# A conditioning dot product for two feature blocks at once: 256 moving columns per product in the first stage of a two-layer diffusion backbone

## The chip, the core and the metric

The kernel runs on one core of a Trainium2 chip. The core has a matrix engine (TensorE, PE in the profile; its weight loads are PEld), an elementwise and reduction engine (VectorE, DVE), an activation engine (ScalarE, ACT), GpSimd (POOL) and SyncE (SP), which here only issues DMAs. They run beside each other and wait for one another by semaphores. The metric is the device time of one execution in microseconds; lower is better.

## The reference

Two layers over 256 latent tokens and 256 context tokens of 2048 features, all in fp32. Each half-layer is modulated by a vector of conditions c (and c_ctx for the context tokens):

```python
sh1, sc1, g1, sh2, sc2, g2 = ada_params(c[:, None, :], ada_w[i], ada_b[i])   # silu(c) @ w + b, in six parts
a  = modulate(h, sh1, sc1)                                                   # h * (1 + scale) + shift
ac = modulate(hc, csh1, csc1)                                                # context: the same weights, c_ctx
q, k, v = jnp.split(a @ w_qkv, 3, axis=-1)                                   # layer 0: neighbourhood attention
```

What matters here is the very beginning: before any key, query or value of layer 0 can be computed, a block of 128 features of the tokens needs its scale (SC1) and shift (SH1): for each of the block's 128 output features a dot product of 2048 terms with silu(c) and another with silu(c_ctx). SC1 and SH1 together are 2 x 2048 x 2048 weights, 32 MB that are read once.

## The kernel before

**Tiling.** The 512 tokens (256 latent, 256 context) are the moving columns, the 2048 features are cut in 16 blocks `kt` of 128. A product of two fp32 matrices is made of three products of rounded parts (`mm3`, L85 to L88): high x high, high x low, low x high; `split_into` (L90) makes the high part on ScalarE (L91) and the low part on VectorE (L92). Weights come through `prefetch` and `piece` (L104, L125): a raw tile (four buffers), then its high and low part (three buffers each).

**The first stage** is the loop over `kt` from L395, about the first 150 us. For each block it adds the block's share to the keys of three heads (`keys`, nine products of 512 columns) and to the values of four heads (`values`, twelve). From `kt` 3 to 14 it also makes an early part of the keys of other heads, twelve products into a bank of their own (`eps`, L444), which VectorE then copies or adds into SBUF (L449, L453). In between, the loop prepares the modulation of a block two ahead (`ahead`): `fetch` loads weights of the conditioning and the block's tokens `xt`; `dots` makes the dot products; `rows` calls `gather`; `modulate` makes tmp = xt * scale + shift on ScalarE (L368) and splits it into `ah` and `al`, the operands of that block's keys and values.

**The dots.** For blocks 0 to 3 TensorE makes both vectors, for blocks 4 to 15 (from `DVE0`) it makes SC1 and VectorE makes SH1. On TensorE (`dot`, L336) the stationary operand is a piece of silu(c) and silu(c_ctx), two columns padded to 32, and the moving one the weights, 128 inputs x 128 outputs; the sixteen products of one block and vector are spread over four strips of 32 columns of the array (`tile_position`) that add up in four groups of 32 partitions of the tile `aps`. `gather` (L349) copies this to SBUF (`row`), adds up the four groups and turns the rows into columns with one small product per vector (L356, with `sel`), and VectorE adds the bias (L358) into `mod`. On VectorE (`dot_dve`, L327) two multiply-and-sum instructions of 128x2048 (L331, for c_ctx and c) and one addition (L334) make SH1 from weights stored the other way round (`ada_s`).

**Buffers and order.** A piece of conditioning weights is 1 MB and takes one of four tiles in turn (`slots`, by the count `n % 4`); its load can be issued when the tile's last reader is done. `aps` and `eps` share one PSUM bank (tag "a", one buffer): each waits until the one before it was read. The order on TensorE in this loop and the loads of `load_st` and `load_x` are fixed in program order (`pin`); from iteration 2 on the loads of `prefetch` are not, and the order of most instructions on VectorE and ScalarE is laid out by the framework's scheduler when the program is built. All loads named here are issued on SP's queue.

Of the kernel before, what the change touches and what calls it, by code (L numbers as in the profile page):

```python
# [2 lines left out]

# [1 line left out]

# [9 lines left out]
ALU = mybir.AluOpType  # L15
# [3 lines left out]
P = 128  # L19
D = 2048  # L20
NT = 256
KT = D // P
# [22 lines left out]
DVE0 = 4  # L45
# [7 lines left out]
def hybrid_kernel(ctx: ExitStack, tc: tile.TileContext, i, out):  # L53
# [213 lines left out]
    with tc.tile_pool(name="attnX", bufs=1) as px, ExitStack() as late:  # L267
# [21 lines left out]
        with tc.tile_pool(name="st", bufs=1) as st:  # L289
# [3 lines left out]
            def load_st(src, name, n):  # L293
                pool, tag, bufs = slots[n % 4]
                r = pool.tile([P, 2048], F32, tag=tag, name=name, bufs=bufs)
                pin(nc.sync.dma_start(r, src))
                return r

            held = {}

            def fetch(kt):
                for t in range(2):
                    src = i["ada_s"][kt - DVE0] if t and kt >= DVE0 else i["ada_p"][kt, t]
                    held[kt, t] = load_st(src, f"ap{kt}{t}", 2 * kt + t)
                load_x(kt)

            zero = st.tile([P, 512], F32, tag="zero", name="zero")
# [16 lines left out]

            raw_c = st.tile([P, KT, 2], F32, tag="rawc", name="raw_c")

            def dot_dve(kt, t):  # L327
                r = held.pop((kt, t))
                junk = outer.tile([P, D], BF16, tag="ada", name=f"junk{kt}", bufs=ADA)
                for n, (o, bc) in enumerate(((junk, cc_bc), (r, c_bc))):  # L330
                    V.scalar_tensor_tensor(  # L331
                        o, r, 1.0, bc, ALU.mult, ALU.mult, accum_out=raw_c[:, kt, 1 - n : 2 - n]
                    )
                V.tensor_scalar(mod[:, 1, kt, :], raw_c[:, kt, :], badj[:, 0, SH1, kt : kt + 1], None, ALU.add)  # L334

            def dot(kt, t):  # L336
                if t and kt >= DVE0:
                    return dot_dve(kt, t)
                if t == 0:
                    dps[kt] = stp_pool.tile([P, 512], F32, tag="a", name=f"aps{kt}")  # L340
                r = held.pop((kt, t))
                for kk in range(KT):
                    g = 32 * (kk % 4)
                    pin(T.matmul(
                        dps[kt][g : g + 32, t * P : (t + 1) * P], c_pad[:, kk, :], r[:, kk * P : (kk + 1) * P],
                        start=kk < 4, stop=kk >= KT - 4, tile_position=(0, g),
                    ))

            def gather(kt):  # L349
                ps = dps.pop(kt)  # L350
                ts = 1 if kt >= DVE0 else 2
                row = st.tile([P, 2 * P], F32, tag="row", name=f"row{kt}", bufs=1)
                S.copy(row[:, 0 : ts * P], ps[:, 0 : ts * P])
                o = ps[:, 256:260].rearrange("p (t b) -> p t b", t=2)
                for t in range(ts):
                    pin(T.matmul(o[:, t, :], row[:, t * P : (t + 1) * P], sel, start=True, stop=True))  # L356
                for t, ada in enumerate((SC1, SH1)[:ts]):
                    V.tensor_scalar(mod[:, t, kt, :], o[:, t, :], badj[:, 0, ada, kt : kt + 1], None, ALU.add)  # L358

            def load_x(kt):  # L360
                xt[kt] = st.tile([P, 512], F32, tag="xt", name=f"xt{kt}", bufs=3)
# [33 lines left out]
            for kt in range(KT):  # L395
                hi, lo = piece()
                first, last = kt == 0, kt == KT - 1

                def keys(h):
                    c = slice(h * P, (h + 1) * P)  # L400
                    mm3(kps[h], hi[:, c], lo[:, c], ah[:, kt, :], al[:, kt, :], first, last, pin)

                def values(b):
                    c, tb = slice(HK0 * P, W0), slice(b * P, (b + 1) * P)
                    mm3(vps[b], ah[:, kt, tb], al[:, kt, tb], hi[:, c], lo[:, c], first, last, pin)

                def dots(k):
                    if k < KT:
                        if k > 2:
                            fetch(k)  # L410
                        for t in range(2):
                            dot(k, t)

                def rows(k):
                    if k < KT:
                        gather(k)

                ahead = kt + 2 if kt > 1 else kt + 1
                keys(0)
                if kt == 2:  # L420
                    rows(3)
                    modulate(3)
                keys(1)
                keys(2)
                dots(ahead)
                values(0)
                values(1)
                rows(ahead)
                values(2)
                values(3)  # L430
                if kt == 0:
                    modulate(1)
                    for bc in (c_bc, cc_bc):
                        pin(S.activation(bc, bc, AF.Silu))
                    fetch(2)
                if kt == 1:
                    modulate(2)
                    dots(3)
                    pos["bufs"], pos["pin"] = 3, False
                for at, h, k0 in EARLY:  # L440
                    if at == kt:
                        h += HK0
                        hi, lo = piece()
                        ps = stp_pool.tile([P, 512], F32, tag="a", name=f"eps{h}{k0}")  # L444
                        for j in range(EN):
                            c = slice(j * P, (j + 1) * P)
                            mm3(ps, hi[:, c], lo[:, c], ah[:, k0 + j, :], al[:, k0 + j, :], j == 0, j == EN - 1, pin)
                        if h in early:
                            V.tensor_tensor(early[h], ps, early[h], ALU.add)  # L449
                        else:  # L450
                            free = NH - 2 * (h - HK0 + 1)
                            early[h] = oT[:, free : free + 2, :].rearrange("p a b -> p (a b)")
                            V.tensor_copy(early[h], ps)  # L453
                if 2 < kt and kt + 1 < KT:
                    modulate(kt + 1)
# [513 lines left out]
    ffn(1, m, (1, G2), "d1", store, free, True)  # L969


def dot_keys():
    keys = []
    for layer, ts in ((0, (SH2, SC2, G1, G2)), (1, (SH1, SC1, G1, SH2, SC2, G2))):
        keys += [(layer, t, nt) for t in ts for nt in range(KT)]
    return keys
# [35 lines left out]
def lay_out(x, c, ctx, c_ctx, ada_w, ada_b, ln_g, ln_b, na_w_qkv, na_w_o, na_rpb,  # L1012
            gm_w_in, gm_ln_g, gm_ln_b, gm_w_s, gm_b_s, gm_w_out, ffn_w_in, ffn_w_out):
    a = {}
    x, ctx = x[0], ctx[0]
    rows = np.stack([c[0], c_ctx])
    a["c_rows"] = rows
    a["c_col"] = rows.reshape(2, KT, P).transpose(2, 1, 0)
    xc = np.concatenate([x, ctx], 0)
    a["xcT"] = xc.T.reshape(KT, P, 512)  # L1020
    a["x_tok"] = x.reshape(2, P, D).transpose(1, 0, 2)
    a["ada_b_col"] = ada_b.reshape(2, 6, KT, P).transpose(3, 0, 1, 2)
    g4, b4 = ln_g.reshape(4, D), ln_b.reshape(4, D)
    a["ln_row"] = np.stack([g4, b4], 1)
    a["ln_col"] = a["ln_row"].reshape(4, 2, KT, P).transpose(3, 0, 1, 2)
    aw = ada_w.reshape(2, D, 6, D)
    dot = np.empty((len(DOT), P, D), np.float32)
    for (layer, t, nt), n in DOT.items():
        dot[n] = aw[layer, :, t, nt * P : (nt + 1) * P].T
    a["ada_t"] = dot  # L1030
    a["ada_p"] = np.stack(
        [[aw[0, :, t, kt * P : (kt + 1) * P].reshape(KT, P, P).transpose(1, 0, 2).reshape(P, 2048)
          for t in (SC1, SH1)] for kt in range(KT)]
    )
    a["ada_s"] = np.stack([aw[0, :, SH1, kt * P : (kt + 1) * P].T for kt in range(DVE0, KT)])
    wq, wk, wv = (na_w_qkv[0][:, n * D : (n + 1) * D] for n in range(3))
    w0 = np.concatenate([wk[:, : HK0 * P], wv[:, :512]], 1)
    a["w_kv0"] = w0.reshape(KT, P, W0)

    a["ident"] = np.eye(P, dtype=np.float32)  # L1040
    a["sel"] = np.tile(np.eye(32, 2, dtype=np.float32), (4, 1))

    a["w_q"] = heads(wq)
    a["w_k"] = heads(wk)[HK0:]
    a["w_v"] = blocks_512(wv)[1:]
    a["bias"] = bias_layout(na_rpb[0])
    a["w_o"] = halves(na_w_o[0])
    parts = ffn_w_in.reshape(2, D, 2, DFF)
    a["w_in_t"] = np.stack([[blocks_512(parts[n, :, p]) for p in range(2)] for n in range(2)])
    a["w_out"] = np.stack([halves(w) for w in ffn_w_out])  # L1050
    a["w_gin"] = blocks_512(gm_w_in[0])
    a["w_gout"] = halves(gm_w_out[0])
    a["gm_row"] = np.stack([gm_ln_g[0], gm_ln_b[0]])
    a["w_s"] = gm_w_s[0].transpose(2, 0, 1)
    a["b_s"] = gm_b_s[0].T
    return {k: np.ascontiguousarray(v) for k, v in a.items()}
# [17 lines left out]
```

## Time and profile before

| what | us |
|---|---|
| median of three runs | 2400.17 (2398.44 to 2400.63) |
| the profiled execution | 2400.89 |
| its span (first to last instruction) | 2399.1 |
| TensorE busy in the first 150 us | 142.93 |
| VectorE busy in the first 150 us | 103.20 |
| DMA share of the first 150 us | 0.92 at 342 GB/s |

Times in the views are from the start of the span; L344 is line 344 of the kernel before. In a row of the timeline stand the start, the length, the engine, the line and operation, out<-in with shapes, how many instructions were merged, and in brackets how long the engine was idle before and what released it. An fp32 product is recorded as two matmuls and two weight loads; a product of the rounded parts is one. Matmuls overlap: the distance from one start to the next says more than the length of one.

### The profile page before, as it was taken

The numbers are of one execution on the slowest core, as the hardware profiler recorded it, in microseconds if no ns is written. First come the engines' busy times: TensorE is split into PE (matmuls) and PEld (weight loads), VectorE is DVE, ScalarE is ACT, GpSimd is POOL, SyncE is SP. The second block draws the span as 40 slices with busy tenths as digits, with TensorE's granted clock in tenths as the row PEclk, the third lists the DMA queues.
The fourth block names the chain that finished last, engine by engine and source line by source line (L and its number), as shares of the span: only waits on it lengthen the run. The fifth ranks groups of instructions, "written<-read, shape, count | busy, mean of one in ns | idle before, by whom it ended". The sixth has DMA issues, their size and how long they took to land.

```text
span 2399.1 us, 31422 instructions
## 1 busy us (share of the span) xinstructions
PE 2370.2 (99%) x11628; PEld 1969.3 (82%) x11628; DVE 1716.8 (72%) x2297; ACT 1121.9 (47%) x1546; POOL 57.4 (2%) x63
## 2 busy tenths in 40 slices
PE   8999999999999999999999999999999999999998
PEld 6788888888788888888888788887788888888886
DVE  4877867677788778788989777686755555556666
ACT  4354434345644444444455554456444444445552
POOL 0000000000010000000000021000100000010000
PEclk9999999999999999999999999999999999999999
DMA  9977677766689899999989555856767666566563
GB/s 392 353 259 244 236 249 241 241 221 210 214 298 349 322 333 335 333 334 342 342 292 341 192 192 196 303 187 208 237 231 234 229 233 223 191 197 200 178 209 132
DMA packets 169106, 614.84 MB, mean 256 GB/s; under 512 B 19604, under 2 KB 21972, under 8 KB 164596
## 3 DMA queue, kind: packets, MB, share of 16 engines
q1 hardware_dynamic: 121172, 440.74, 53.6%
q10 hardware_dynamic: 46372, 167.86, 19.8%
q0 software_dynamic: 1408, 4.23, 0.6%
q8 instruction: 91, 1.49, 0.2%
q14 instruction: 63, 0.52, 0.1%
HBM read 610.62 MB, written 2.13 MB: 255 GB/s over the span
## 4 chain that ended last, share of the span: by engine, by line
PE 95%; DVE 2%; ACT 1%; DMA 1%; issue 1%; SPq 0%; POOL 0%; DVEq 0%; ACTq 0%; POOLq 0%
PE pu L87 7%; PE pu L88 7%; PE pu L86 7%; PE pod L86 7%; PE pod L87 6%; PE pod L88 6%; PE pg L88 6%; PE pg L86 6%; PE pg L87 6%; PE vps L86 2%; PE vps L88 2%; PE vps L87 2%; PE kps L87 2%; PE kps L88 2%; PE kps L86 2%; PE qps L86 1%
## 5 line engine op out<-in xcount | busy, mean ns | idle before, releaser
L92 DVE TENSOR_TENSOR lwf<-rwf,hwf 128x1024 fp32r<-128x1024 f32 x320 | 392.1, 1225 | 282.3 <-ACT hwf L91 281.8
L91 ACT CAST hwf<-rwf 128x1024 fp32r<-128x1024 f32 x320 | 336.2, 1051 | 483.7 <-PE pu L88 221.5
L150 DVE SCALAR_TENSOR_TENSOR ad<-ad,c_bc 128x1024 f32<-128x1024 f32 x320 | 388.0, 1219 | 0.0
L86 PE MATMUL pod<-hwd,ghd 128*128 128x512 f32 x684 | 266.5, 390 | 0.0
L87 PE MATMUL pod<-lwd,ghd 128*128 128x512 f32 x684 | 266.3, 389 | 0.0
L88 PE MATMUL pod<-hwd,gld 128*128 128x512 f32 x684 | 265.9, 389 | 0.0
L92 DVE TENSOR_TENSOR lwd<-rwd,hwd 128x1024 fp32r<-128x1024 f32 x172 | 212.1, 1234 | 63.0 <-ACT hwd L91 62.6
L91 ACT CAST hwd<-rwd 128x1024 fp32r<-128x1024 f32 x172 | 180.4, 1049 | 68.5 <-PE pod L88 45.1
L86 PEld LDWEIGHTS pod<-hwd,ghd 128*128 128x128 f32 x684 | 128.4, 188 | 27.0 <-DVE sg L847 0.3
L88 PEld LDWEIGHTS pod<-hwd,gld 128*128 128x128 f32 x684 | 128.4, 188 | 26.7
L87 PEld LDWEIGHTS pod<-lwd,ghd 128*128 128x128 f32 x684 | 128.4, 188 | 26.3
L86 PE MATMUL pg<-hwf,f0h 128*128 128x512 f32 x320 | 126.5, 395 | 0.0
L86 PE MATMUL pg<-hwf,f1h 128*128 128x512 f32 x320 | 126.5, 395 | 0.0
L88 PE MATMUL pg<-hwf,f0l 128*128 128x512 f32 x320 | 124.8, 390 | 0.0
L88 PE MATMUL pg<-hwf,f1l 128*128 128x512 f32 x320 | 124.7, 390 | 0.0
L86 PE MATMUL pu<-hwf,f1h 128*128 128x512 f32 x320 | 124.6, 389 | 0.0
L86 PE MATMUL pu<-hwf,f0h 128*128 128x512 f32 x320 | 124.6, 389 | 0.0
L88 PE MATMUL pu<-hwf,f1l 128*128 128x512 f32 x320 | 124.5, 389 | 0.0
L88 PE MATMUL pu<-hwf,f0l 128*128 128x512 f32 x320 | 124.5, 389 | 0.0
L87 PE MATMUL pu<-lwf,f1h 128*128 128x512 f32 x320 | 124.5, 389 | 0.0
L87 PE MATMUL pg<-lwf,f0h 128*128 128x512 f32 x320 | 124.5, 389 | 0.0
L87 PE MATMUL pu<-lwf,f0h 128*128 128x512 f32 x320 | 124.5, 389 | 0.0
(346 smaller groups left out, 5137.1 us busy)
## 6 DMA issues: line engine op xcount, KB each, us to landing
ad<-in_ada_t ACTq DMA_DIRECT2D x320, 512.0 KB
rwf<-in_w_in_t SPq DMA_DIRECT2D x320, 512.0 KB
rwd<-in_w_out SPq DMA_DIRECT2D x176, 512.0 KB
rwg<-in_w_gin SPq DMA_DIRECT2D x64, 512.0 KB
ap<-in_ada_p SPq DMA_DIRECT2D x20, 1024.0 KB
rwq<-in_w_q SPq DMA_DIRECT2D x32, 512.0 KB
rwo<-in_w_o SPq DMA_DIRECT2D x32, 512.0 KB
rwt<-in_w_in_t SPq DMA_DIRECT2D x32, 512.0 KB
```

Source lines behind the costliest of these rows:

```text
L86: keep(T.matmul(ps, sh, mh, start=first, stop=False))
L87: keep(T.matmul(ps, sh, ml, start=False, stop=False))
L88: keep(T.matmul(ps, sl, mh, start=False, stop=last))
L91: S.copy(hi, src)
L92: V.tensor_tensor(lo, src, hi.bitcast(F32), ALU.subtract)
L150: pin(V.scalar_tensor_tensor(r, r, 1.0, c_bc[:, half * 1024 : (half + 1) * 1024], ALU.mult, ALU.mult, accum_out=o[:, nt : nt + 1],))
```

## The change

TensorE's conditioning products become 256 columns wide. For blocks 0 to 3 one product covers SC1 and SH1 of a block; for blocks 4 to 15 one product covers SC1 of two neighbouring blocks, so that only the even iterations have dots on TensorE, a copy to `row` and a gather. The weights `ada_p` are laid out anew: a piece of 1 MB holds half of the 2048 inputs for 256 outputs, where before it held all inputs for 128 outputs. `fetch` loads both halves when the pair begins, then the shift piece of the block itself; the tiles are taken in the order of the loads. Outputs and the number and size of the loads are the same.

```diff
+            loads = count()
+
             def fetch(kt):
-                for t in range(2):
-                    src = i["ada_s"][kt - DVE0] if t and kt >= DVE0 else i["ada_p"][kt, t]
-                    held[kt, t] = load_st(src, f"ap{kt}{t}", 2 * kt + t)
+                if kt < DVE0 or kt % 2 == 0:
+                    for half in range(2):
+                        src = i["ada_p"][group(kt), half]
+                        held[kt, half] = load_st(src, f"ap{kt}{half}", next(loads))
+                if kt >= DVE0:
+                    held[kt, 2] = load_st(i["ada_s"][kt - DVE0], f"ap{kt}2", next(loads))
                 load_x(kt)
...
-            def dot(kt, t):
-                if t and kt >= DVE0:
-                    return dot_dve(kt, t)
-                if t == 0:
+            def dot(kt, half):
+                if half == 0:
                     dps[kt] = stp_pool.tile([P, 512], F32, tag="a", name=f"aps{kt}")
-                r = held.pop((kt, t))
-                for kk in range(KT):
-                    g = 32 * (kk % 4)
+                r = held.pop((kt, half))
+                for kk in range(KT // 2):
+                    k, g = half * (KT // 2) + kk, 32 * (kk % 4)
                     pin(T.matmul(
-                        dps[kt][g : g + 32, t * P : (t + 1) * P], c_pad[:, kk, :], r[:, kk * P : (kk + 1) * P],
-                        start=kk < 4, stop=kk >= KT - 4, tile_position=(0, g),
+                        dps[kt][g : g + 32, 0:NT], c_pad[:, k, :], r[:, kk * NT : (kk + 1) * NT],
+                        start=k < 4, stop=k >= KT - 4, tile_position=(0, g),
                     ))
 
             def gather(kt):
                 ps = dps.pop(kt)
-                ts = 1 if kt >= DVE0 else 2
                 row = st.tile([P, 2 * P], F32, tag="row", name=f"row{kt}", bufs=1)
-                S.copy(row[:, 0 : ts * P], ps[:, 0 : ts * P])
+                S.copy(row, ps[:, 0:NT])
                 o = ps[:, 256:260].rearrange("p (t b) -> p t b", t=2)
-                for t in range(ts):
+                for t in range(2):
                     pin(T.matmul(o[:, t, :], row[:, t * P : (t + 1) * P], sel, start=True, stop=True))
-                for t, ada in enumerate((SC1, SH1)[:ts]):
-                    V.tensor_scalar(mod[:, t, kt, :], o[:, t, :], badj[:, 0, ada, kt : kt + 1], None, ALU.add)
+                for t, (ada, k) in enumerate(vectors(kt)):
+                    V.tensor_scalar(mod[:, (SC1, SH1).index(ada), k, :], o[:, t, :], badj[:, 0, ada, k : k + 1], None, ALU.add)
...
                     if k < KT:
                         if k > 2:
                             fetch(k)
-                        for t in range(2):
-                            dot(k, t)
+                        for half in range(2):
+                            if (k, half) in held:
+                                dot(k, half)
+                        if k >= DVE0:
+                            dot_dve(k)
 
                 def rows(k):
-                    if k < KT:
+                    if k in dps:
                         gather(k)
...
+def group(kt):
+    return kt if kt < DVE0 else (kt + DVE0) // 2
+
+
+def vectors(kt):
+    return ((SC1, kt), (SH1, kt)) if kt < DVE0 else ((SC1, kt), (SC1, kt + 1))
```

More of the change, by code (lines that the diff above doesn't have):

```diff
@@ L2 @@
 from functools import partial
+from itertools import count
 import numpy as np
@@ L325, in hybrid_kernel, with dot_dve @@
             raw_c = st.tile([P, KT, 2], F32, tag="rawc", name="raw_c")
-            def dot_dve(kt, t):
-                r = held.pop((kt, t))
+            def dot_dve(kt):
+                r = held.pop((kt, 2))
                 junk = outer.tile([P, D], BF16, tag="ada", name=f"junk{kt}", bufs=ADA)
@@ L334, in dot_dve @@
                 V.tensor_scalar(mod[:, 1, kt, :], raw_c[:, kt, :], badj[:, 0, SH1, kt : kt + 1], None, ALU.add)
-            def dot(kt, t):
-                if t and kt >= DVE0:
-                    return dot_dve(kt, t)
-                if t == 0:
+            def dot(kt, half):
+                if half == 0:
                     dps[kt] = stp_pool.tile([P, 512], F32, tag="a", name=f"aps{kt}")
-                r = held.pop((kt, t))
-                for kk in range(KT):
-                    g = 32 * (kk % 4)
+                r = held.pop((kt, half))
+                for kk in range(KT // 2):
+                    k, g = half * (KT // 2) + kk, 32 * (kk % 4)
                     pin(T.matmul(
-                        dps[kt][g : g + 32, t * P : (t + 1) * P], c_pad[:, kk, :], r[:, kk * P : (kk + 1) * P],
-                        start=kk < 4, stop=kk >= KT - 4, tile_position=(0, g),
+                        dps[kt][g : g + 32, 0:NT], c_pad[:, k, :], r[:, kk * NT : (kk + 1) * NT],
+                        start=k < 4, stop=k >= KT - 4, tile_position=(0, g),
                     ))
@@ L1030, in lay_out @@
     a["ada_t"] = dot
[L1031 to L1034, printed above, removed]
+    a["ada_p"] = np.stack([
+        np.concatenate([aw[0, :, t, k * P : (k + 1) * P] for t, k in vectors(kt)], 1)
+        .reshape(2, KT // 2, P, 2 * P).transpose(0, 2, 1, 3).reshape(2, P, D)
+        for kt in range(KT) if kt < DVE0 or kt % 2 == 0
+    ])
     a["ada_s"] = np.stack([aw[0, :, SH1, kt * P : (kt + 1) * P].T for kt in range(DVE0, KT)])
```

## The prediction

> **What bounds the kernel now.** First the page: how full each engine is, and where the chain of work that ended last runs.
>
> ```profile
> span 2399.1 us, 31422 instructions
> PE 2370.2 (99%) x11628; PEld 1969.3 (82%) x11628; DVE 1716.8 (72%) x2297; ACT 1121.9 (47%) x1546; POOL 57.4 (2%) x63
> PE 95%; DVE 2%; ACT 1%; DMA 1%; issue 1%; SPq 0%; POOL 0%; DVEq 0%; ACTq 0%; POOLq 0%
> ```
>
> TensorE is the bound: it is busy for 2370.2 of 2399.1 us and carries 95% of the chain, so only 28.9 us can be won from its waits. The change lies in the first 150 us, so next comes the busy time by stretches there (columns: stretch, its length, busy time of each engine with its number of instructions, granted clock, DMA share, GB/s).
>
> ```profile
> 34.00:49.00 15.00, 13.50 (x114) 10.22 (x114) 10.92 (x15) 5.88 (x12) 0.00 (x0) 1.00 1.02 414
> 67.00:76.00 9.00, 9.00 (x69) 7.18 (x68) 7.70 (x11) 3.48 (x7) 0.00 (x0) 1.00 0.94 335
> ```
>
> There are two regimes. Up to some 49 us the DMA engines are full (414 GB/s) and TensorE still waits: 1.5 us of these 15. Later TensorE is never idle (9.00 of 9.00) and DMA has room. In the first regime it matters which bytes come when; in the second only TensorE's own work, as long as VectorE (7.70 of 9.00) keeps up.
>
> **What TensorE pays for the dots.** The timeline around a double dot (block 2: two vectors, 32 products) and around a single one (block 7: one vector, 16 products; the profile records each fp32 product as two matmuls, so x64 and x32):
>
> ```profile
> 25.25 0.39 PE L88 MATMUL kps<-ah,lkv 128*128 128x512 f32 x1
> 25.57 1.96 PE L344 MATMUL aps<-ap,c_pad 128*32 128x128 f32 x64
> ...
> 27.79 0.40 PE L87 MATMUL vps<-lkv,ah 128*128 128x512 f32 x1
> ...
> 61.76 0.39 PE L88 MATMUL kps<-ah,lkv 128*128 128x512 f32 x1
> ...
> 62.08 1.08 PE L344 MATMUL aps<-ap,c_pad 128*32 128x128 f32 x32
> ...
> 63.43 0.40 PE L87 MATMUL vps<-lkv,ah 128*128 128x512 f32 x1
> ```
>
> From the last product of keys to the second of values is 1.67 us around the single dot. Two ordinary steps of 0.23 us (the distance of full products in this stage) belong to the others, so the single dot costs 1.21. In the same way the double one costs 2.54 - 0.46 = 2.08. So 32 records add 0.87, and some 0.34 us is paid once for each visit: entering and leaving the 32-column form.
>
> The diff keeps the columns: a pair is 16 products of 256 columns instead of 2 x 16 of 128. The records' spacing is (1.96 - 0.27)/63 = 27 ns, four strips at once, so 107 ns in one strip for 128 columns. Is that columns or a price for each start? Full-array fp32 products of 256 columns answer:
>
> ```profile
> 11.41 1.54 PE L382 MATMUL vps<-zero 128*128 128x256 f32 x6
> ```
>
> The spacing of these six is about (1.54 - 0.45)/5 = 0.22 us, twice 107 ns. So time goes by columns; 256 of them in a strip cost about 215 ns, and a pair 8 x 0.215 = 1.72 against 16 x 0.107 = 1.71. Merging the products by itself gains nothing I can see. The trace has no product of this form with 256 columns, so the ends are: 0.87 a pair if only starts cost (rival c), and 32 x 0.215 = 6.9 if four strips no longer ran side by side; nothing in the form changes but the columns, and at 128 they do run so, which excludes the latter. I take 1.72, that is zero difference, nearest to the row above. What goes is a visit for each pair: 0.34 us, six times (pairs 4/5 to 14/15).
>
> [...]
>
> **The gather.** After a pair it has two products into the block's bank (four records) instead of one.
>
> ```profile
> 28.71 0.40 PE L88 MATMUL vps<-hkv,al 128*128 128x512 f32 x1
> 28.95 0.50 PE L356 MATMUL aps<-sel,row 128*128 128x2 f32 x4
> ...
> 29.63 0.39 PE L87 MATMUL vps<-lkv,ah 128*128 128x512 f32 x1
> ...
> 64.35 0.40 PE L88 MATMUL vps<-hkv,al 128*128 128x512 f32 x1
> ...
> 65.04 0.39 PE L87 MATMUL vps<-lkv,ah 128*128 128x512 f32 x1
> ```
>
> Less two ordinary steps: 0.92 - 0.46 = 0.46 for the double, 0.69 - 0.46 = 0.23 for the single. Twice 0.23 against 0.46: nothing. ScalarE's row copy grows once instead of being made twice, and VectorE's two additions per pair stay two; both engines have idle time here. The DMAs are as many and as large as before (20 of ada_p, 12 of ada_s, 1 MB each).
>
> **What moves.** Pair 4/5 needs both its 1 MB halves before values of iteration 2 can go on, where before one 1 MB piece was enough. The chain of waits, then the timeline:
>
> ```profile
> 26.71 9.19 DMA ap<-in_ada_p
> ```
>
> ```profile
> 36.03 1.08 PE L344 MATMUL aps<-ap,c_pad 128*32 128x128 f32 x32 [0.46 <-DMA ap<-in_ada_p]
> ...
> 39.00 2.28 DVE L331 SCALAR_TENSOR_TENSOR junk<-ap,oT 128x2048 bf16<-128x2048 f32 x1
> ...
> 41.99 0.39 PE L88 MATMUL kps<-ah,lkv 128*128 128x512 f32 x1
> ...
> 42.83 1.08 PE L344 MATMUL aps<-ap,c_pad 128*32 128x128 f32 x32 [0.45 <-DMA ap<-in_ada_p]
> ...
> 43.54 1.08 DVE L92 TENSOR_TENSOR lkv<-rkv,hkv 128x896 fp32r<-128x896 f32 x1
> ...
> 44.80 1.09 ACT L368 ACTIVATE tmp<-xt,mod 128x256 f32<-128x256 f32 x2 [3.49 <-DVE mod L334]
> ...
> 45.12 0.39 PE L88 MATMUL vps<-hkv,al 128*128 128x512 f32 x1
> ...
> 46.09 0.30 PEld L356 LDWEIGHTS aps<-sel,row 128*128 128x128 f32 x2 [1.01 <-ACT row L353]
> ...
> 46.65 0.39 PE L87 MATMUL vps<-lkv,ah 128*128 128x512 f32 x1
> ...
> 49.54 0.68 DVE L92 TENSOR_TENSOR lwe<-rwe,hwe 128x512 fp32r<-128x512 f32 x1
> ...
> 52.36 0.39 PE L88 MATMUL kps<-ah,lkv 128*128 128x512 f32 x1
> ...
> 53.09 1.08 PE L344 MATMUL aps<-ap,c_pad 128*32 128x128 f32 x32 [0.34 <-DVE oT L453]
> ```
>
> The first piece of block 4 lands at 35.9 us. The queue is full, so the next megabyte (the second half) comes 1.05 MB / 414 GB/s = 2.5 us later, at 38.5. The first half's products end near 36.9: TensorE stands **1.6 us** longer. Against that go two stalls of block 5: its dot waited for DMA (41.99 to 42.83 is 0.84, where 0.32 is usual: **0.5**), and its gather waited for ScalarE's row copy, stuck behind modulate(4) (1.53 - 0.46 = 1.07, where 0.23 is usual: **0.85**). Both leave iteration 3 with the dot. With the merged visit (0.34) the front is 1.6 - 0.5 - 0.85 - 0.34 = -0.1 us when the early key product of iteration 3 begins.
>
> The next meeting is dot(6). Before, it began at 53.09 after a wait of 0.73 - 0.32 = 0.4 for VectorE's copy of the early bank, which the dots share; without any wait it would now begin at 52.6. The piece for VectorE's own dot of block 4 comes third now instead of second, at 38.5 + 2.5 = 41.0 instead of before 39.0. From the first VectorE dot (39.00) to its modulation (44.80) are 5.8 us: 46.8. If VectorE's two passes for block 5 (2.3 each: 39.00 to 43.54 for two) follow at once, with al and the low half of the next early weights between them (0.6 each from start to start: 0.68 in the row at 49.54), its copy ends at 46.8 + 2.3 + 0.6 + 0.6 + 2.3 + 0.7 = 53.3, and the dot starts some 0.3 after, at 53.6. That is **+0.5** against 53.09. If VectorE instead waits for al(4) first, it is some 2 us later; if the copy goes ahead of the second dot, 0.5 earlier than before.
>
> **The steady loop** (iteration 6, all VectorE work of one period):
>
> ```profile
> 71.05 0.81 PEld L344 LDWEIGHTS aps<-ap,c_pad 128*32 128x32 f32 x32 [0.35 <-DVE mod L334]
> ...
> 72.71 0.69 DVE L92 TENSOR_TENSOR al<-tmp,ah 128x512 fp32r<-128x512 f32 x1 [0.82 <-ACT ah L91]
> ...
> 73.88 0.22 DVE L358 TENSOR_SCALAR mod<-aps,badj 128x2 f32<-128x2 f32 x1 [0.48 <-PE aps L356]
> ...
> 79.04 0.69 DVE L453 COPY oT<-eps 128x512 f32<-128x512 f32 x1
> ...
> 79.77 1.09 DVE L92 TENSOR_TENSOR lkv<-rkv,hkv 128x896 fp32r<-128x896 f32 x1
> ...
> 80.02 0.81 PEld L344 LDWEIGHTS aps<-ap,c_pad 128*32 128x32 f32 x32 [0.35 <-DVE mod L334]
> ```
>
> Dots start every 8.97 us (62.08, 71.05, 80.02). TensorE's own sum is 33 products x 0.23 + 1.21 + 0.23 = 9.0; but VectorE's loop closes just as tightly: the copy ends at 79.73, the dot starts 0.29 later. For a pair TensorE needs 17.94 - 0.34 = **17.6**. VectorE's way round: from the pair's dot to its additions 2.83 (71.05 to 73.88) + 0.87 + 0.3 for the second vector = 4.0; then 5.85 to the end of the even copy, 0.1 + 1.0 for lkv, 0.6 for al and 5.7 to the end of the odd copy, and 0.3: about 17.6. It is level, if VectorE doesn't wait for al; with the wait of 0.82 it is **18.4**.
>
> **The sum.** The likeliest: +0.5 at dot(6), then five more visits merged, 5 x -0.34 = -1.7: **-1.2 us**. Against the profiled execution (2400.89 us, of which 2399.1 are the span) that is 2399.7; the median of the runs, 2400.17, is 0.7 lower, so I forecast 2399.0, **2399**. A measurement of this kernel can tell about 0.2% (4.8 us) from no change, and this is less.
>
> **Rivals.**
> (a) VectorE sets the period, mildly: +2.4 at dot(6) (it waited for al(4)), four periods from dot(6) to dot(14) at +0.46, -0.34 at the end: +3.9, **2404**. For it: the copy already ends only 0.3 us ahead of the dot. Against: iteration 5 and its odd fellows have no gather and no dot, so VectorE may run ahead there.
> (b) Slower: in odd iterations VectorE also makes the low half of the next weights (lkv, 1.0 us) ahead of the bank's copy. The place is dot(6), (8) to (14), which wait for the shared bank; the price is 1.0 at each of five on top of (a): +8.9, **2409**. It decides once more than 13.3 us (17.6 - 4.0 - 0.3) pass on VectorE from the pair's additions to the odd copy's end.
> (c) Each start has a price and columns don't: a pair's 32 records would cost 0.87, not 1.74, and a first block's 0.87 as well: 10 x 0.87 = 8.7 beside the 1.2: **2390**. The six records of 256 columns speak against it. [...]
> (d) The order turns out well everywhere (copy ahead of the second dot from the start): 1 us better than the forecast, **2398**; still no difference that shows.
>
> **How the numbers follow.** The forecast with (d) 0.5, (a) 0.32, (b) 0.12, (c) 0.06. Forecast, (d) and (a) lie within 0.2%: 0.82 the same; (b) gives slower 0.12, (c) faster 0.06. The range reaches from 2396.5 (a little beyond (d), for the columns' 0.02 to 0.2 a pair) to 2405 (a little past (a)); (b) and (c) are left out, 0.18 together.
>
> **What would show it.** Right: dots of pairs as x32 records of 256 columns lasting about 1.95 us each, not 1.08; a stall near 1.6 us in TensorE before the second half of pair 4; no wait for ScalarE's row copy near 45 us; pair dots 17.6 us apart. Wrong: pair dots over 18 us apart with VectorE's copy of the early bank as releaser (a, b); pair dots lasting near 1.1 us (c). If the later 2,250 us come out in another order on any engine, that is outside this sum.

## The result, and the profile after

The changed kernel takes 2411.56 us (median of five runs, 2408.24 to 2418.25) against 2400.17 (2398.44 to 2400.92) for the kernel before: a ratio of 1.0053, 95% interval 1.0036 to 1.0070. It is about 11 us slower, outside the range of the prediction. The execution that was profiled is the longest of the five (2418.25), so its lines are read for the first stage only, and single events behind that stage with care.

The head of the page, and the stretches of the first stage that the prediction showed of before (stretch, length, busy time of each engine, granted clock, DMA share, GB/s), with two short ones added:

```profile
span 2416.5 us, 30782 instructions
PE 2378.4 (98%) x11308; PEld 1967.9 (81%) x11308; DVE 1718.3 (71%) x2297; ACT 1123.0 (46%) x1540; POOL 55.6 (2%) x63
```

```profile
34.00:49.00 15.00, 14.86 (x98) 10.99 (x91) 10.22 (x15) 6.20 (x11) 0.00 (x0) 1.00 1.01 410
67.00:76.00 9.00, 6.96 (x36) 4.58 (x38) 6.05 (x10) 3.01 (x5) 0.00 (x0) 0.81 0.88 329
73.00:75.00 2.00, 2.00 (x5) 1.09 (x4) 0.54 (x1) 0.00 (x0) 0.00 (x0) 0.50 0.93 382
131.00:133.00 2.00, 2.00 (x6) 1.36 (x5) 0.69 (x1) 0.04 (x1) 0.00 (x0) 0.50 0.97 367
```

TensorE has 320 matmul records fewer and is busy 8.2 us longer. Up to 49 us it fares better than before (14.86 of 15.00 busy, 13.50 before). The stretch from 67 to 76 us, which was full (9.00), now holds 6.96, and its granted clock, 1.00 before, is 0.81; between 73 and 75 it is 0.50. The same happens near 132. What stands before the low clock is a wait. TensorE's timeline there:

```profile
69.25 0.39 PE L87 MATMUL kps<-ah,hkv 128*128 128x512 f32 x1
71.68 0.50 PE L88 MATMUL kps<-al,hkv 128*128 128x512 f32 x1 [2.04 <-DVE al L93]
...
72.33 0.63 PE L87 MATMUL kps<-ah,hkv 128*128 128x512 f32 x1
72.76 0.63 PE L88 MATMUL kps<-al,hkv 128*128 128x512 f32 x1
...
74.47 0.63 PE L89 MATMUL kps<-ah,lkv 128*128 128x512 f32 x1
75.03 2.17 PE L348 MATMUL aps<-ap,c_pad 128*32 128x256 f32 x32
```

The second key product of iteration 6 needs `al`, the low half of block 6's modulated tokens. It starts 2.43 us behind the first, where 0.23 is usual: **2.20 us lost**. Then the products start 0.43 apart instead of 0.23. From the second product to the dot are 3.35 us; at full clock they are seven steps of 0.23 and the 0.32 ahead of a dot, 1.93. So the low clock costs **1.42 us** more. Why `al` is late is to be seen on ScalarE and VectorE:

```profile
65.09 0.62 ACT L92 CAST ah<-tmp 128x512 fp32r<-128x512 f32 x1
```

```profile
64.83 2.29 DVE L337 SCALAR_TENSOR_TENSOR junk<-ap,oT 128x2048 bf16<-128x2048 f32 x1
...
67.39 0.69 DVE L93 TENSOR_TENSOR lwe<-rwe,hwe 128x512 fp32r<-128x512 f32 x1 [0.27 <-ACT hwe L92]
68.00 2.29 DVE L337 SCALAR_TENSOR_TENSOR ap<-ap,c_bc 128x2048 f32<-128x2048 f32 x1
...
70.21 0.69 DVE L459 COPY oT<-eps 128x512 f32<-128x512 f32 x1
70.81 0.22 DVE L340 TENSOR_SCALAR mod<-raw_c,badj 128x2 f32<-128x2 f32 x1
70.94 0.69 DVE L93 TENSOR_TENSOR al<-tmp,ah 128x512 fp32r<-128x512 f32 x1
```

What `al` reads is ready at 65.7. VectorE is never idle for long, but in its queue `al` of block 6 stands behind both passes of block 7's shift, the bank's copy and the shift's addition, and runs at 70.94. Before, `al` of a block ran ahead of the first pass of the next, with the gather's addition between them (the prediction's rows at 72.71 and 73.88 show it for blocks 7 and 8). Block 7 has no gather any more.

Later in the same iteration the second effect shows, first on VectorE, then on TensorE:

```profile
79.26 0.22 DVE L361 TENSOR_SCALAR mod<-aps,badj 128x2 f32<-128x2 f32 x1 [5.72 <-PE aps L359]
79.39 2.28 DVE L337 SCALAR_TENSOR_TENSOR junk<-ap,oT 128x2048 bf16<-128x2048 f32 x1
...
81.60 0.21 DVE L361 TENSOR_SCALAR mod<-aps,badj 128x2 f32<-128x2 f32 x1
```

```profile
80.24 0.40 PE L89 MATMUL vps<-hkv,al 128*128 128x512 f32 x1
81.96 0.47 PE L87 MATMUL eps<-ah,hwe 128*128 128x512 f32 x1 [1.32 <-DVE mod L361]
```

A pair's gather has two additions, and the scheduler put the first pass of the shift between them. The bank of `aps` is free only when both have read it, so the early key product waits: 1.72 from start to start, 1.49 over the usual.

A third, smaller loss lies ahead of both. Dot 6 starts 1.82 us behind the last key product, where 0.32 is usual (0.73 in the kernel before), because VectorE's copy of the early bank stands behind both passes of block 5 and runs only at 53.10:

```profile
53.84 1.93 PE L348 MATMUL aps<-ap,c_pad 128*32 128x256 f32 x32 [1.43 <-DVE oT L459]
```

The first two effects come back one more time (waits for `al` near 127, for the addition near 138). Over the whole first stage, in starts on TensorE read from the profile of each kernel (us; the first query product stands for the end of the stage):

| | first key product | dot 4 | dot 6 | dot 8 | dot 10 | dot 12 | dot 14 | first query product |
|---|---|---|---|---|---|---|---|---|
| before | 13.83 | 36.03 | 53.09 | 71.05 | 89.00 | 106.95 | 124.89 | 153.78 |
| after | 15.49 | 37.08 | 53.84 | 75.03 | 94.52 | 112.07 | 133.40 | 163.67 |

9.89 us are lost by the end of the stage. From dot 6 to 8 it is 21.19, where merged visits were to give 17.6; the wait and the low clock, 2.20 + 1.42, are the difference of 3.6. From 8 to 10 it is 19.49: the dot itself still runs 0.24 longer at the low clock, and the early product waits 1.49. The same pair of losses follows at 12 to 14 and behind 14. The undisturbed interval, 10 to 12, is 17.55.

In this execution some 7 us more were lost behind the stage, around one event of the second stage:

```profile
679.97 0.80 PE L88 MATMUL pu<-lwt,f0h 128*128 128x512 f32 x1 [3.76 <-DVE lwt L93]
```

It varies with the execution: the second profile of the same kernel, below, has 1.41 us from start to start there instead of 4.14, and that of narrow_between has 4.86, in an execution of 2406.95 us, while the median of that kernel is 2400.72.

### The profile page after: what moved, and what is told of

It is laid out like the page before. It is cut to its first block, busy times and chain, and to the rows that moved or that the text cites. A ratio compares the mean times of both kernels' runs of the same rounds, so it can differ in the third digit from the quotient of the medians.

```text
span 2416.5 us, 30782 instructions
## 1 busy us (share of the span) xinstructions
PE 2378.4 (98%) x11308; PEld 1967.9 (81%) x11308; DVE 1718.3 (71%) x2297; ACT 1123.0 (46%) x1540; POOL 55.6 (2%) x63
## 4 chain that ended last, share of the span: by engine, by line
PE 79%; issue 15%; DVE 3%; ACT 1%; DMA 1%; POOL 0%; DVEq 0%; SPq 0%; POOLq 0%; ACTq 0%
PE pod L87 6%; PE pod L89 6%; PE pod L88 6%; PE pu L88 6%; PE pu L89 6%; PE pu L87 6%; PE pg L87 6%; PE pg L89 6%; PE pg L88 6%; PE vps L87 1%; PE vps L89 1%; PE vps L88 1%; PE gu L89 1%; PE gu L88 1%; PE gu L87 1%
```

## The experiments

The theory after this reading: the order of the queue on VectorE costs the time, through the late `al` first, through the split additions second; the 256 columns themselves cost nothing. The rivals: it was this execution; wide products cost something; the merging of pairs costs something whatever the order (a fuller wait for DMA, VectorE as the bound). `issue_after(x)` puts what its block records behind `x` in the queue of x's engine.

**The same kernel again.**

> The changed kernel once more. Order theory (the lost time comes from the order in which VectorE's instructions are issued, which is laid down in the program): the first stage ends again some 8 to 10 us late (first query product near 162 to 164 us instead of 153.8), TensorE waits again for al near 69 and near 127 us, 2.2 us each, and the two early products after them wait 1.5 us each for the second addition. Chance theory (it was an accident of one execution): these waits are gone or elsewhere. The 7 us lost near 676 us in the first look are outside both; if they are gone, the total is near 2409 to 2411.

2411.69 us (2409.55 to 2413.84), ratio 1.0046 (1.0028 to 1.0063). The same four waits: 2.42 and 2.43 us from start to start for `al` at 70.4 and 127.1, 1.72 twice for the addition at 79.8 and 138.1; the first query product at 163.28. The loss is in the program and not in one execution. One thing differs. Behind the first wait for `al` the clock stayed at 1.00 this time:

```profile
72.81 0.50 PE L88 MATMUL kps<-al,hkv 128*128 128x512 f32 x1 [2.04 <-DVE al L93]
...
74.86 0.42 PE L348 MATMUL aps<-ap,c_pad 128*32 128x256 f32 x4
```

From the late product to the dot it is 2.05 us instead of 3.35, and from dot 6 to dot 8 19.88 instead of 21.19. So 1.3 us is the price of the low clock alone. (This execution came 1.14 us later to the wait, the first key product of iteration 6 at 70.39 against 69.25, so little of that shows at the end of the stage: 163.28 against 163.67.)

**al_between: `al` ahead of the second pass.** In odd blocks the second pass is queued behind `al` of the block before.

```diff
-            dot_dve(k)
+            dot_dve(k, (0,) if k > DVE0 and k % 2 else (0, 1))
...
-            modulate(kt + 1)
+            low = modulate(kt + 1)
+            if kt % 2 and kt + 2 < KT:
+                with tc.issue_after(low):
+                    dot_dve(kt + 2, (1,))
```

> The changed kernel, with VectorE's second pass of an odd block queued behind the low half al of the even block. Order theory: no wait for al at blocks 6 and 12, no drop of the clock after it, and since the two additions then stand together again, no wait of the early products; pair dots 17.6 to 17.9 us apart; total 2398 to 2402. Pairing theory (VectorE's work for two blocks no longer fits between two pair dots, whatever its order): pair dots 18.4 us apart or more with VectorE's bank copy as releaser, total 2404 to 2408. Width theory (256-column products cost TensorE more): total stays near 2411.

2400.91 us (2397.91 to 2408.8, 12 runs), ratio 1.0003 (0.9994 to 1.0011): the loss is gone. With that one constraint VectorE's queue came out the same for every pair from block 6 on, with the additions together too. At block 5 the bank's copy now runs ahead of the second pass (50.60, the pass 51.20), and dot 6 starts at 52.19 without a wait. So this run undoes all three losses at once and does not tell them apart. From dot 8 on its pair dots stand 17.72 apart, and in the first such interval the clock is 1.00 and TensorE full:

```profile
71.17:88.89 17.72, 17.62 (x103) 13.70 (x103) 15.24 (x22) 6.95 (x11) 0.00 (x0) 1.00 0.95 354
```

The first query product starts at 152.80, 0.98 us earlier than in the kernel before. That is about the size the prediction's sum had (-1.2), though not by the sum's terms (more on this below), and it is too small for the time of a run to show. One wait remains that no step had foreseen:

```profile
56.74 0.61 PE L363 MATMUL aps<-sel,row 128*128 128x2 f32 x4 [1.02 <-ACT row L360]
```

```profile
54.42 0.22 DVE L344 TENSOR_SCALAR mod<-raw_c,badj 128x2 f32<-128x2 f32 x1
```

```profile
54.67 1.09 ACT L375 ACTIVATE tmp<-xt,mod 128x256 f32<-128x256 f32 x2 [3.79 <-DVE mod L344]
55.80 0.62 ACT L92 CAST ah<-tmp 128x512 fp32r<-128x512 f32 x1
56.32 0.37 ACT L360 COPY row<-aps 128x256 f32<-128x256 f32 x1
```

The gather of pair 6 waits for ScalarE's row copy, which stands behind `tmp` and `ah` of block 5, and these wait for VectorE's shift addition at 54.42. It is the stall of 45 us in the kernel before, come back in another iteration.

**narrow_between: the same order, 128 columns.** Pairs are still visited together and the order is that of al_between, but every product has 128 columns again, twice as many of them.

```diff
-                for kk in range(KT // 2):
-                    k, g = half * (KT // 2) + kk, 32 * (kk % 4)
+                for k in range(KT):
+                    g = 32 * (k % 4)
-                        dps[kt][g : g + 32, 0:NT], c_pad[:, k, :], r[:, kk * NT : (kk + 1) * NT],
+                        dps[kt][g : g + 32, half * P : (half + 1) * P], c_pad[:, k, :], r[:, k * P : (k + 1) * P],
```

> The same as al_between, but every product 128 columns wide again (32 products for a pair, each 1 MB piece a block's vector over all inputs). Order theory: the pair's section on TensorE is as long as with 256 columns (2.05 to 2.10 us), and the total equals that of al_between within 1.5 us. Width theory: this kernel is faster than al_between by several us. A price for each start would make it slower by up to 9 us.

2400.72 us, ratio 1.0007 (0.9999 to 1.0016); pair dots 17.74, 17.73 and 17.73 apart; the first query product at 152.83. The dots of one pair in al_between, then here:

```profile
71.17 1.93 PE L352 MATMUL aps<-ap,c_pad 128*32 128x256 f32 x32
73.04 0.50 PE L87 MATMUL vps<-hkv,ah 128*128 128x512 f32 x1
```

```profile
71.12 1.95 PE L352 MATMUL aps<-ap,c_pad 128*32 128x128 f32 x64
73.01 0.50 PE L87 MATMUL vps<-hkv,ah 128*128 128x512 f32 x1
```

From the first dot to the next product it is 1.87 with 32 records and 1.89 with 64. The width is worth 0.02 us a pair: time goes by columns.

**adds_first: only the additions together.** The passes of an even block are queued behind both additions of its pair; where `al` comes is left to the scheduler.

```diff
                     if k in dps:
-                        gather(k)
+                        add = gather(k)
+                        if k >= DVE0:
+                            with tc.issue_after(add):
+                                dot_dve(k)
```

> The changed kernel with VectorE's passes for an even block queued behind the gather's two additions; in this order al stands behind both passes of the odd block at blocks 6, 10 and 14. Order theory: three waits for al of 2.2 us, each followed by about 3 us at half clock (1.5 us lost), and no wait of the early products: total 2408 to 2413, as the changed kernel. If the split additions were the main loss: 2403 or less. Pairing theory: 2404 to 2408.

2409.01 us (2405.83 to 2414.89), ratio 1.0037 (1.0024 to 1.0050). No wait for an addition is left, but now there are three for `al`, each 2.42 from start to start (68.8, 107.8 and 145.2). The first of them, and the clock behind it (behind the second it stayed at 1.00, from 110.5 to 113 us):

```profile
71.17 0.50 PE L88 MATMUL kps<-al,hkv 128*128 128x512 f32 x1 [2.03 <-DVE al L93]
```

```profile
73.00:76.00 3.00, 3.00 (x26) 1.19 (x29) 0.03 (x1) 0.00 (x0) 0.00 (x0) 0.51 0.94 344
```

The first query product starts at 162.17. With the additions in order most of the loss is still there: dot 6 waits for the bank's copy as in the changed kernel (1.43 us idle), and behind it the waits for `al` are the only ones of over 1.2 us. A loss of this size needs no split additions. This order has three late `al` where the changed kernel has two, so the run does not measure how the changed kernel's loss divides; that kernel's own trace does, with 2.20 + 1.42 at the first late `al` against 1.49 at the addition.

**late_al: the kernel before with two late `al`.** Nothing is merged and nothing widened; `al` of blocks 6 and 12 is queued behind both passes of blocks 7 and 13. The second edit only holds the rest of VectorE's order in place.

```diff
-                    modulate(kt + 1)
+                    held_back = kt + 2 in (7, 13)
+                    with tc.issue_after(passed[kt + 2]) if held_back else nullcontext():
+                        modulate(kt + 1)
...
-                        gather(k)
+                        add = gather(k)
+                        if k >= DVE0:
+                            with tc.issue_after(add):
+                                dot(k, 1)
```

> The kernel before, with its narrow products and one block at a time; only al of the blocks 6 and 12 is queued behind both passes of the blocks 7 and 13, as the changed kernel has it. Theory (the order of al, not the width of the products, costs the time): two TensorE gaps of about 2.3 to 2.5 us near 69.4 and 123, the clock at half for about 3.4 us behind each, so 3.5 to 4 us lost at each; the first query product at about 161 instead of 153.78, time about 2408, ratio about 1.003. Rival (such a wait is made up in the iteration behind it, and the loss of the changed kernel comes with the merged pairs): gaps there, but the first query product within 2 us of 153.78 and a ratio within 0.001 of 1.

2409.32 us (2407.05 to 2410.91), ratio 1.0030 (1.0018 to 1.0041). The narrow kernel now shows the picture of the changed one: VectorE, then TensorE, then the clock behind both waits (stretches as above):

```profile
68.04 2.29 DVE L333 SCALAR_TENSOR_TENSOR ap<-ap,c_bc 128x2048 f32<-128x2048 f32 x1
...
70.98 0.69 DVE L92 TENSOR_TENSOR al<-tmp,ah 128x512 fp32r<-128x512 f32 x1
```

```profile
69.11 0.39 PE L86 MATMUL kps<-ah,hkv 128*128 128x512 f32 x1
71.72 0.71 PE L87 MATMUL kps<-al,hkv 128*128 128x512 f32 x1 [2.22 <-DVE al L92]
```

```profile
73.00:75.00 2.00, 2.00 (x6) 1.32 (x4) 0.58 (x1) 0.00 (x0) 0.00 (x0) 0.50 0.98 401
...
130.50:132.50 2.00, 2.00 (x6) 1.61 (x5) 0.79 (x2) 0.29 (x1) 0.00 (x0) 0.50 0.98 406
```

Dot 6 starts at 53.29 (53.09 in the kernel before), dot 8 at 75.33 (71.05), dot 14 at 133.19 (124.89), the first query product at 162.12 (153.78). So each late `al` costs 4.1 us (4.28 - 0.20, and about as much at the second), 2.38 of them the wait (2.61 less 0.23), and nothing of it is made up later. The rival that such a wait is won back in the next iteration falls.

**row_first: the row copy ahead of the next block.** Made from al_between, against the wait at 55 us.

```diff
-                rows(ahead)
+                copied = rows(ahead)
...
-                    low = modulate(kt + 1)
+                    with tc.issue_after(copied) if copied is not None else nullcontext():
+                        low = modulate(kt + 1)
```

> As al_between, and in the even iterations from 4 on ScalarE's tmp and ah of the next block are queued behind the row copy of the pair's gather. Theory (TensorE's 1.42 us gap at 55.3 in al_between is the row copy standing behind tmp and ah, which wait for VectorE's shift addition): the gap before the gather near 55 falls to about 0.25, the copy starts at about 54.1, the pairs of dots stay 17.7 apart, and the second stage's first query product starts at about 151.6 instead of 152.80; time about 2399.5, ratio to the kernel before about 0.9995. Rival (VectorE sets the period, so that what TensorE gains there it waits for later): gap gone, but the first query product still at 152.8, and a wait for al or for the bank copy in the iterations 6 to 13 that al_between does not have.

2400.0 us (2397.14 to 2403.47), ratio 0.9993 (0.9984 to 1.0002). The gap at 55 is gone, and yet the first query product starts at 152.84, as in al_between. Mine was the wrong theory here and the rival right: the pair dots are now 17.96 to 18.02 apart, and VectorE's bank copy releases them:

```profile
88.43 1.93 PE L352 MATMUL aps<-ap,c_pad 128*32 128x256 f32 x32 [0.35 <-DVE oT L460]
```

```profile
92.41 0.34 DVE L365 TENSOR_SCALAR mod<-aps,badj 128x2 f32<-128x2 f32 x2 [2.90 <-PE aps L363]
92.67 0.68 DVE L93 TENSOR_TENSOR al<-tmp,ah 128x512 fp32r<-128x512 f32 x1
93.27 2.28 DVE L339 SCALAR_TENSOR_TENSOR junk<-ap,oT 128x2048 bf16<-128x2048 f32 x1
...
105.65 0.69 DVE L460 TENSOR_TENSOR oT<-eps,oT 128x512 f32<-128x512 f32 x1
```

With the row copy moved ahead of `tmp` and `ah`, ScalarE ends the odd block's `ah` only at 92.45 (90.74 in al_between), when the pair's additions can run too, and `al` stands behind them. In al_between it filled VectorE's wait for the gather; here VectorE idles 2.90 us and then makes it, 0.6 us that all later work of the pair stands behind. VectorE's way round is then some 18.0, over TensorE's 17.7.

**scalar_order: the start as it was.** As row_first, and ScalarE casts the first weight block before it writes `tmp` of block 0.

```diff
-            modulate(0)
+            with tc.issue_after(cast[0]):
+                modulate(0)
```

> As row_first, and ScalarE casts the first weight block before it writes tmp of block 0, as it did in the kernel before. Theory: the first key product starts 0.84 us earlier than it would (about 13.65 instead of 14.49 in al_between), but the second half of the pair 4/5 does not land earlier for that, so the wait in the dots of pair 4 grows from 1.38 to about 2.0 to 2.2 and the first query product stays where row_first has it, near 151.6; time within 1 us of row_first. If that longer wait halves the clock as the 2.42 us waits of the changed kernel did, it costs about 1.3 us more. Rival (the start is on the path that sets the end): the first query product at about 150.8, time 0.8 us below row_first.

2401.67 us (2397.74 to 2403.79), ratio 0.9999 (0.9990 to 1.0008). The first key product comes 0.91 us earlier than in row_first (13.59). The first query product comes 0.52 earlier (152.32), between the two theories: the wait in the dots of pair 4 did not grow (1.71 from start to start, 1.66 in row_first), because that load itself landed 0.50 earlier; both had left that out. No version beats the kernel before by more than a measurement can tell.

**wide_first: 256 columns in blocks 0 to 3 alone**, where nothing is merged.

```diff
+                if kt < DVE0:
+                    for kk in range(KT // 2):
+                        k, g = t * (KT // 2) + kk, 32 * (kk % 4)
...
+                            dps[kt][g : g + 32, 0:NT], c_pad[:, k, :], r[:, kk * NT : (kk + 1) * NT],
```

> The kernel before, with 256 moving columns only in the dots of the blocks 0 to 3, where nothing is merged. Theory (the width is free; the change loses 0.84 us at the start because ScalarE's order has the first weight cast between the two halves of tmp): gather to first key product 3.7 us instead of 2.88, the wait for loads in the dots of blocks 4 and 5 shrinks by about as much, dots of block 6 and all later ones within 0.3 us of the kernel before; time within 1 us of it. Rival (256 columns cost more or less per product than two of 128): the dots of the blocks 1 to 3 last other than twice 0.65 us, the first query product moves by that times four, over 0.5 us.

2401.61 us (2399.65 to 2405.0), ratio 1.0002 (0.9993 to 1.0011). The double dots last as before (1.95 for block 1), and from the gather to the first key product it is 3.72 us, not 2.88, as expected. That is ScalarE's order:

```profile
12.05 0.60 ACT L376 ACTIVATE tmp<-xt,mod 128x256 f32<-128x256 f32 x1 [1.14 <-DVE mod L366]
12.56 0.92 ACT L91 CAST hkv<-rkv 128x896 fp32r<-128x896 f32 x1
13.38 0.60 ACT L376 ACTIVATE tmp<-xt,mod 128x256 f32<-128x256 f32 x1
```

But I expected dot 6 within 0.3 us of the kernel before, and it is 1.78 late (54.87), as is everything after it (query product 155.56). Beyond the 0.84, the clock fell to 0.50 behind this kernel's wait ahead of its first key products, and the waits for loads swallowed only a part of the delay (the dots of block 1 start 2.33 late, those of block 4 still 1.76):

```profile
16.00:19.00 3.00, 3.00 (x12) 1.87 (x13) 0.00 (x0) 0.00 (x0) 0.00 (x0) 0.50 1.04 423
```

## Why the prediction was wrong

**TensorE's columns: right.** Pair dots are x32 records of 1.93 us where 1.95 was named; narrow_between puts the width at 0.02 us a pair. Rival (c), a price for each start, is refuted: 64 records instead of 32 cost 0.02 us a pair.

**The visit and the gather: right, within about 0.1 us.** 0.34 less for each pair gave 17.6 for TensorE; where nothing else intrudes, the intervals are 17.55 (after) and 17.72 (al_between).

**The front.** The stall for the second half of pair 4, named at 1.6, is 1.00 us (al_between) and 1.28 (row_first) in the kernels that reach dot 4 at 36.06, where the prediction had it at 36.03. In the changed kernel TensorE came 1.05 us later to dot 4 and so waited only some 0.36 (its dots last 2.29 instead of 1.93). The row copy's stall near 45 went, as said; in al_between it returned at 55. The chain to dot 6 held for the order that it assumed: the bank's copy was to end at 53.3 and the dot to start at 53.6, and in the changed kernel, which has this order, the copy ends at 53.79 and the dot starts at 53.84. Not in the sum at all was the start: the first key product 1.66 later, of which 0.84 is ScalarE's changed order (wide_first has it without the merging). The other 0.8 are the first dots, which took 1.94 and 1.52 us in that execution where wide_first took 1.07 for each; the last section comes back to them.

**The step that failed** is the one on VectorE's order in the odd iterations. The prediction wrote under rival (a): "iteration 5 and its odd fellows have no gather and no dot, so VectorE may run ahead there", and counted that in favour of no loss; and in the steady loop: "It is level, if VectorE doesn't wait for al". Both ask whether VectorE is kept waiting. The trace of after shows the opposite: VectorE ran ahead, into work that nobody needed yet, and TensorE waited for the small `al` behind it. For the odd blocks the sum put `al` between the passes once, at block 5, and carried it to all pairs without asking what would hold it there. Before, the odd block's gather lay in between: its addition stood behind `al` and ahead of the passes in VectorE's queue, for every block from 4 on. The change took that gather away. This allowed the new order and did not force it: in the changed kernel `al` of blocks 4 and 10 still came between the passes of the next block (49.55 and 107.72), and `al` of blocks 6, 8, 12 and 14 behind both; TensorE waited for those of 6 and 12. al_between, whose one constraint puts `al` back between the passes, returns 10.87 us of the first stage (1.65 of them by dot 6, of which 1.00 is the start, which varies); late_al, which only takes it out of its place in the old kernel, loses 8.1 from dot 6 on.

**A price missing beside it.** Any wait was priced at its length. Here 2.20 us of waiting cost 3.6 (changed kernel) and 2.38 cost 4.1 (late_al) where the clock fell behind it.

**Rivals (a) and (b)** were near in time (2404 and 2409) but not in place: their mark, the bank copy as releaser of the pair dots, occurs only at dot 6 of the changed kernel (1.43 us). row_first does show (a): VectorE sets the period, at 17.96 to 18.02.

al_between, with `al` where the sum had it, ends the stage 0.98 us earlier than the kernel before, and 2400.91 us against 2400.66 is no difference, as forecast. That its 0.98 lies so near the sum's 1.2 is in part luck. Dot 6 starts 0.90 earlier than before, where the sum had 0.5 later (the bank's copy goes ahead of the second pass there, as rival (d) had it). With the row copy's stall, which was not in the sum, the stretch from dot 6 to dot 8 is 1.02 longer than before (18.98 against 17.96). Behind dot 8 four merged visits bring 1.10, where 4 x 0.34 = 1.36 was named.

Open: the medians of the changed kernel lie 11 us over the kernel before and its stage 9.5 to 9.9; the rest of some 1.5 us is within what executions vary. The two traced executions lost 7.5 and 3.5 us behind the stage, and one of median length was not traced. No run has the split additions alone. Why the scheduler chose this order was not looked into; what it did to the time is shown.

## What to carry to other kernels

When a change takes away a wait, look at what stood around it in the helper engine's queue: without it the order may come out anew when the program is built, and a long instruction with no hurry may then stand ahead of a short one that the critical engine needs. Price the queue of the helper engines by "who waits for what stands behind this", not by their busy time (VectorE was busy for 6.05 of the 9 us in which it made TensorE wait). One pinned edge per pair of blocks, here the second pass behind `al`, made the difference between 0.5% slower and even.

## What the runs showed of the hardware

**A wait can cost the clock, and not every wait does.** Nine waits for `al` were traced in four executions, 2.42 to 2.61 us from start to start. Behind six of them the granted clock fell to 0.50: both of after (71.68 and 129.91), the second of after_again (0.50 from 130 to 133), the first of adds_first (0.51 from 73 to 76), both of late_al (0.50 from 73 to 75 and from 130.5 to 132.5). Behind two it stayed at 1.00: the first of after_again (72.7 to 76) and the second of adds_first (110.5 to 113); behind the third of adds_first it was not read. So one and the same wait of the same program cost the clock in one execution and not in the other.

At 0.50 the products of after stood 0.43 us apart instead of 0.23. Its two stretches of low clock in this stage lasted 3.41 us each (72.15 to 75.57 and 130.18 to 133.59) and began 0.47 and 0.27 us behind the late product. In adds_first more time passed: the late product is at 71.17, the steps from 71.51 to 72.44 are still 0.22 to 0.24, and only behind that come 0.33 and 0.43.

Shorter waits of after left the clock alone: the one of 1.82 us from start to start ahead of dot 6 and the two of 1.72 for the additions were not followed by a fall (1.00 from 12 to 72.15, from 75.57 to 130.18 and from 133.59 to 164). Ahead of the first key product TensorE was idle for 1.71 us in after and for 1.72 in wide_first; the clock was 1.00 behind it in after (15 to 18) and 0.50 in wide_first (16 to 19). What decides between the two was not shown: no run moved a wait to try it.

**The start varies too.** The changed kernel's first dots took 1.94 us for a piece of one megabyte where wide_first took 1.07 (after, then wide_first), at a granted clock of 1.00 in both (6 to 9 us and 6 to 10 us):

```profile
6.73 1.94 PE L348 MATMUL aps<-ap,c_pad 128*32 128x256 f32 x16 [0.77 <-DMA ap<-in_ada_p]
```

```profile
6.87 1.07 PE L345 MATMUL aps<-ap,c_pad 128*32 128x256 f32 x16 [1.12 <-DMA ap<-in_ada_p]
```

al_between and adds_first have the same products there, and ScalarE's row copy, which waits for them, was idle for 7.19 and 7.01 us before it, against 8.41 in after and 8.3 in after_again. So up to 1 us at the start does not come with the form of the dots; what it comes with was not shown.
